# The last output pair and the first two feed-forward blocks issued in written order on ScalarE and VectorE

## The chip, the cores and the metric

One core of one Trainium2 chip runs the whole layer in one launch. The metric is the device time of an execution in microseconds; the times before are 1346.68, 1347.53 and 1349.25 us, median 1347.53.

## The reference

One encoder layer on 1024 tokens of width 1024, all in float32. After two kinds of attention and a gated sum, the part that matters here is:

```python
x = x + y @ w_out                                    # the "output" product
h = rms_norm(x, norm_ffn)
u = silu(h @ w_gate) * (h @ w_up)                    # 2816 hidden columns
x = x + u @ w_down
```

## The kernel before

**Products.** Each float32 operand is split in two: `split` lets ScalarE round the source to the fast matmul type (the high part, line 50 or, with a scale, 53) and VectorE subtract (the low part, line 51 or 54). A product is three matmuls, high x high, high x low and low x high (lines 788 to 790). Two 256-wide pieces of weights are multiplied at once by a Strassen-Winograd scheme with seven products, numbered 1 to 7 (class `Seven`). Each product is one `step`: 12 matmuls of 128x512. A step needs its weights (`prepare`: a sum of weight quarters on VectorE, line 765, then a split) and four token operands `mv[p][0..3]`. Its result goes to one of four PSUM banks X, Y, V and Z. Steps 1 and 6 end with a ScalarE copy of one bank into the next (line 792), because later steps add onto that copy: Y is copied to Z after step 6, and steps 7, 3 and 4 follow, 7 and 4 into Z and 3 into Y.

**Output pairs.** `out_pair(i)`, i = 0 to 3, computes 256 rows of x @ w_out in order 1, 5, 6, 2, 7, 3, 4 (pair 0 in another order). It adds the banks to two residual rows `r[i,0]` and `r[i,1]` (lines 1074 and 1096), stores them to x1_dram and adds up squares for the norm. It also makes the token sums that the feed-forward products take (`TokenSums`: t1, t2, t3 early, t4 in `rest`). Their two buffers hold one pair at a time, so the sums of pairs 0 to 2 go to f_dram, six rows of 256 KB each. Four buffers of tag e4 hold the residual rows of two pairs less one, and the running squares. The rows of pair i+1 are loaded in step 4 of pair i, one before and one after the six stores.

**Feed-forward blocks.** `hidden(i)`, 22 of them, each takes one 128-column piece of w_gate and w_up through the same seven steps. Blocks 0 and 1 run interleaved in order 1, 5, 6, 7, 3, 2, 4. After step 6 of both, `ffn_norm` sums the squares on TensorE, VectorE and GpSimd make 1/rms, and after step 7 `spread_norm` spreads it over the partitions. Their token operands for products 5, 6, 7, 3, 2 and 4 (that is `BACK`, index n) are made by `feed(n, j)`, j being the pair: j < 3 is fetched from f_dram into the low half of the operand's slot and split there, j = 3 is split from the sums on chip. `first_feeds` issues the twelve fetches of n = 0 to 3 in step 2 of pair 3; n = 4 and 5 follow after the pair. Slots have tags: products 5 and 6 take U slots (used before by the output operands 1 and 5), 7 and 3 take V slots (before: 6 and 2), 2 and 4 take H slots (before: 7, 3, 4).

**Order of issue.** TensorE follows the written order throughout. `dma` keeps all loads and stores of these stages in written order on the SyncE queue, which waits in turn for each slot or value. ScalarE and VectorE follow a planner that reorders by estimated times; in step 2 of pair 3 the weights of products 1 and 5 of blocks 0 and 1 get a higher priority.

Of the kernel before, what the change touches and what calls it, by code (L numbers as in the profile page):

```python
# [25 lines left out]
def block_kernel(ctx, tc, x, xt, small, w_in, rpb, t5, w_ba, w_bb, w_out, w_gate, w_up, w_down,  # L26
                 onehot, swmask, namask, out):
    nc = tc.nc
    P = 128
# [15 lines left out]
    def f(ap):  # L45
        return ap.bitcast(F32)

    def split(hi, lo, src, eng=None, scale=None):
        if scale is None:
            a = nc.scalar.copy(hi, src)  # L50
            b = (eng or nc.vector).tensor_tensor(lo, src, f(hi), ALU.subtract)  # L51
        else:
            a = nc.scalar.activation(hi, src, AF.Copy, scale=scale)
            b = nc.vector.scalar_tensor_tensor(lo, src, scale, f(hi), op0=ALU.mult, op1=ALU.subtract)
        return a.ins, b.ins
# [18 lines left out]
    def operand(tag, nm):  # L74

        z = big.tile([P, 2, 512], F32R, tag=tag, name=nm, bufs=16 if tag == "H" else 8)
        return z[:, 0, :], z[:, 1, :]
# [9 lines left out]
    def dma(dst, src):  # L87

        tc.keep_in_program_order(nc.sync.dma_start(dst, src))
# [4 lines left out]
    def half_cols(h):  # L94
        return slice(h * 512, h * 512 + 512)

    def tok(t):
        return slice(t * P, (t + 1) * P)
# [74 lines left out]
    f_dram = drp.tile([18 * P, 512], F32, name="f_dram")  # L173
# [303 lines left out]
    with tc.tile_pool(name="at", bufs=1) as ap:  # L477
# [144 lines left out]
        n = len(steps)  # L622
# [40 lines left out]
        for gi, (kind, _) in enumerate(order):  # L663
            m = 8 * group_columns(*order[gi])[1]
            lo, hi = due[gi], due[gi + 1]
# [35 lines left out]
    ORDER = (1, 5, 6, 2, 7, 3, 4)  # L701
# [6 lines left out]
    def scratch(nm):  # L708
        return hp.tile([P, 512], F32, tag="S", name=nm, bufs=2)
# [4 lines left out]
    def scratch2(nm):  # L714
        return hp.tile([P, 1024], F32, tag="e4", name=nm, bufs=4)
# [12 lines left out]
    def in_turn(*gens):  # L728
        gens = list(gens)
        while gens:  # L730
            gens = [g for g in gens if next(g, gens) is not gens]

    def bank_sets():

        return [{b: bank(RING[4 * i + n], f"bank{b}{i}") for n, b in enumerate("XYVZ")} for i in range(2)]
# [133 lines left out]
    sets = bank_sets()  # L869
# [77 lines left out]
    sets = bank_sets()  # L947
# [12 lines left out]
    for n, (d, half) in enumerate(turns):  # L960
        j, c = d // 2, half_cols(half)
# [15 lines left out]
        if half == 0:  # L977
            p = 2 if d % 2 else 1
# [4 lines left out]
            elif d == 7:  # L983
                my[7], my[3] = ([operand("H", f"y{p}_{i}") for i in range(4)] for p in (7, 3))
                for m, q in enumerate((7, 3)):
                    for i in range(3):
                        hi, lo = my[q][i]
                        row = (3 * m + i) * P
                        dma(f(lo), y_dram[row:row + P, :])
                        split(hi, lo, f(lo))  # L990
        elif d % 2:
            (b11, b12), (b21, b22) = halves(y[d - 1]), halves(y[d])
            t = TokenSums(f"y{j}", b11, b12, b22).rest(b21)
# [3 lines left out]
            for m, p in enumerate((7, 3, 4)):  # L997
                row = (3 * m + j) * P
# [7 lines left out]
    for q in (7, 3, 4):  # L1006
        for i in range(4) if q == 4 else (3,):
            hi, lo = my[q][i]
            if i < 3:
                row = (6 + i) * P  # L1010
# [3 lines left out]
    hid = {}  # L1014

    def prefetch_ffn(i):

        if i >= NF:
            return prefetch_down(i - NF)
        st = [w_stage(f"wg{i}_"), w_stage2(f"wu{i}_")]  # L1020
        for t, w in zip(st, (w_gate, w_up)):
            dma(t.rearrange("p (k c) -> p k c", c=P), w[0, :, tok(i)].rearrange("(k p) c -> p k c", p=P))
        hid[i] = Seven(f"f{i}", [two(z) for z in st], 4, mx, sets)
# [18 lines left out]
    mx = {1: [operand("H", f"f1_{j}") for j in range(4)]}  # L1042
    r = {}

    def out_row(i, a):
        r[i, a] = scratch2(f"r{i}_{a}")
        dma(r[i, a], xt[tok(2 * i + a), :])
# [4 lines left out]
    raw_t = {}  # L1052
    pairs = {0: loads}
    BACK = (5, 6, 7, 3, 2, 4)

    def feed(n, j):

        hi, lo = mx[BACK[n]][j]
        src, scale = raw_t[j][BACK[n]]
        if j < 3:  # L1060
            row = (3 * n + j) * P
            dma(f(lo), f_dram[row:row + P, :])
            src = f(lo)
        split(hi, lo, src, scale=scale)

    def out_pair(i, order, then={}):
        s = pairs[i]
        ra = r[i, 0], r[i, 1]
        x, y, v, z = (s.banks[b] for b in "XYVZ")
        ga, gb = (gffn[:, 2 * i + a:2 * i + a + 1] for a in range(2))  # L1070

        def done(a, half, bank_):
            c = half_cols(half)
            nc.vector.tensor_add(ra[a][:, c], bank_, ra[a][:, c])
            dma(x1_dram[tok(2 * i + a), c], ra[a][:, c])

        def squares(a, half):
            c = half_cols(half)
            if i or (a, half) not in ((0, 0), (1, 1)):
                sq = scratch(f"sq{i}_{a}_{half}")  # L1080
                nc.scalar.activation(sq, ra[a][:, c], AF.Square)
                nc.vector.tensor_add(both_sums[:, c], both_sums[:, c], sq)
            else:
                nc.scalar.activation(both_sums[:, c], ra[a][:, c], AF.Square)

        for p in order:
            s.prepare(p)
        for p in order:
            s.step(p)
            if p == 2:  # L1090
                done(0, 0, x)
                split(*mx[1][i], ra[0][:, LO], scale=ga)
                squares(0, 0)
            elif p == 5:
                for a in range(2):
                    nc.vector.tensor_add(ra[a][:, HI], v, ra[a][:, HI])
            elif p == 7:
                done(1, 1, z)
                squares(1, 1)
            elif p == 3:  # L1100
                done(0, 1, y)
                t = raw_t[i] = TokenSums(f"x{i}", ra[0][:, LO], ra[0][:, HI], ra[1][:, HI], ga, gb)
                if i == 3:
                    for n in range(4):
                        feed(n, 3)
                squares(0, 1)
            elif p == 4:
                done(1, 0, z)
                t.rest(ra[1][:, LO])
                if i < 3:  # L1110
                    out_row(i + 1, 0)
                    for n, q in enumerate(BACK):
                        row = (3 * n + i) * P
                        dma(f_dram[row:row + P, :], t[q][0])
                    out_row(i + 1, 1)
                squares(1, 0)
            then.get(p, lambda: None)()

    def prefetch_out(i):
        pairs[i] = out_loads(i)  # L1120

    def first_feeds():
        for n in range(4):
            mx[BACK[n]] = [operand("UUVV"[n], f"f{BACK[n]}_{j}") for j in range(4)]
            for j in range(3):
                feed(n, j)

    prefetch_out(1)
    for i in range(3):
        order = ORDER if i else FIRST  # L1130
        out_pair(i, order, {order[3]: lambda: prefetch_out(i + 2) if i < 2 else prefetch_ffn(0)})
    def lead_in():
        prefetch_ffn(1)
        with tc.high_priority(offset=400):
            for p in (1, 5):
                for i in range(2):
                    hid[i].prepare(p)
        first_feeds()

    out_pair(3, ORDER, {2: lead_in})  # L1140


    mv = mx
    for n in (4, 5):
        mx[BACK[n]] = [operand("H", f"f{BACK[n]}_{j}") for j in range(4)]
        for j in range(4):
            feed(n, j)

    rsb = wide_rs

    def ffn_norm(half, ss):

        for j in range(4):
            nc.tensor.matmul(ss[:, j:j + 1], both_sums[:, tok(4 * half + j)], ones[:, 0:1], start=True, stop=True)
        rs = hp.tile([P, 4], F32, tag="rs", name=f"rs{half}", bufs=2)
        nc.vector.tensor_scalar(rs, ss[:, 0:4], 1.0 / D, EPS, op0=ALU.mult, op1=ALU.add)  # L1156
        nc.gpsimd.tensor_tensor(rs, rs, mhalf[:, 0:4], ALU.pow)  # L1157
        dg = scratch(f"dg{half}")
        for j in range(4):
            nc.vector.tensor_scalar_mul(dg[:, tok(j)], ident, rs[:, j:j + 1])  # L1160
        return dg

    def spread_norm(half, dg, rb):
        for j in range(4):
            nc.tensor.matmul(rb[:, tok(j)], ones, dg[:, tok(j)], start=True, stop=True)
        nc.scalar.copy(rsb[half], rb)
# [42 lines left out]
            nc.sync.dma_start(u_dram[row:row + P, :], t[p][0])  # L1209

    ga, gb = (hidden(i, LAST2) for i in range(2))
    for g in (ga, gb, ga, gb, ga, gb):
        next(g)
    dg = [ffn_norm(half, sets[half]["V"]) for half in range(2)]
    next(ga)
    next(gb)
    for half in range(2):
        spread_norm(half, dg[half], sets[half]["V"])
    in_turn(ga, gb)
    for i in range(2, NF - 2):  # L1220
        run(hidden(i))
# [6 lines left out]
    for ch, (k0, n) in enumerate(CHUNKS):  # L1228
        for q, p in enumerate(ORDER):
            for j in range(n):  # L1230
                hi, lo = mv[p][j]
                row = (7 * (k0 + j) + q) * P
# [92 lines left out]
```

## Time and profile before

| | us |
|---|---|
| median of three runs | 1347.53 |
| profiled execution | 1350.09 |
| its span, first to last instruction | 1348.30 |
| TensorE busy in the span | 1316.1 |
| VectorE, ScalarE busy | 1005.4, 673.4 |

The span is what the rows below are measured in; 1.79 us of the profiled execution lie outside it. The profiled execution is 2.56 us above the median of the three runs. Times of a row are counted from the span's start. TensorE has work for 98% of the span, so a time saved is an idle stretch of TensorE filled, or a stretch at its lower clock brought to the higher.

### The profile page before, as it was taken

How to read it: one execution, taken by the hardware profiler on the slowest of the kernel's cores; microseconds unless marked ns; L12 is line 12 of the kernel's file. 1: busy time of each engine (PE TensorE's matmuls, PEld its weight loads, DVE VectorE, ACT ScalarE, POOL GpSimd, SP SyncE). 2: the span in 40 equal slices, each digit the busy share in tenths (PEclk: the TensorE clock that was granted, in tenths of full speed). 3: DMA queues.
4: the chain of work that ended last, by engine and by line, in shares of the span. 5: the costliest groups of instructions: out<-in, count | busy, mean ns of one | idle time of the engine just before them, and what ended most of it. 6: DMA issues, size and time to landing. Idle time of an engine off the chain costs nothing.

```text
span 1348.3 us, 19145 instructions
## 1 busy us (share of the span) xinstructions
PE 1316.1 (98%) x6464; PEld 1132.6 (84%) x6464; DVE 1005.4 (75%) x1989; ACT 673.4 (50%) x1381; POOL 170.6 (13%) x308
## 2 busy tenths in 40 slices
PE   9999999999999999999997999999999999999998
PEld 8999999999887887887885888888888888888887
DVE  5678878887769736768978867766667679797775
ACT  7567857776645224535555433333333347263432
POOL 1354645563210000000000000000000000000000
PEclk9999999999999999999998999999999999999999
DMA  9431312142514436657783433223333346682542
GB/s 327 120 86 41 95 54 82 44 116 55 170 66 152 141 94 202 202 176 226 241 288 105 132 101 102 86 88 109 117 118 111 96 139 225 243 262 65 165 133 86
DMA packets 177571, 184.03 MB, mean 136 GB/s; under 512 B 20496, under 2 KB 125968, under 8 KB 177472
## 3 DMA queue, kind: packets, MB, share of 16 engines
q1 hardware_dynamic: 177216, 182.70, 42.9%
q8 instruction: 51, 0.84, 0.3%
q14 instruction: 48, 0.39, 0.1%
q10 hardware_dynamic: 256, 0.10, 0.0%
HBM read 128.74 MB, written 48.97 MB: 132 GB/s over the span
## 4 chain that ended last, share of the span: by engine, by line
PE 84%; DVE 7%; DMA 4%; ACT 3%; issue 2%; SPq 1%; POOL 0%; ACTq 0%; DVEq 0%; POOLq 0%
PE bankZ L788 6%; PE bankZ L790 6%; PE bankZ L789 6%; PE bankY L790 5%; PE bankY L788 5%; PE bankY L789 5%; PE bankX L789 5%; PE bankX L790 5%; PE bankX L788 5%; PE pj L317 4%; PE pj L316 4%; PE pj L315 4%; PE bankV L789 3%; PE o L602 3%; PE bankV L790 3%; PE bankV L788 3%
## 5 line engine op out<-in xcount | busy, mean ns | idle before, releaser
L552 ACT ACTIVATE E<-E,nm 128x384 f32<-128x384 f32 (+3 forms) x128 | 75.7, 591 | 51.6 <-DVE nm L546 46.0
L554 POOL TENSOR_SCALAR E<-E,nm 128x384 f32<-128x384 f32 (+1 forms) x128 | 78.1, 611 | 101.3 <-DVE nm L553 72.0
L51 DVE TENSOR_TENSOR pl<-tp,ph 128x384 fp32r<-128x384 f32 (+1 forms) x128 | 66.3, 518 | 13.4 <-ACT ph L50 12.2
L50 ACT CAST ph<-tp 128x384 fp32r<-128x384 f32 (+1 forms) x128 | 57.4, 449 | 21.6 <-PE tp L564 20.6
L51 DVE TENSOR_TENSOR f<-f 128x512 fp32r<-128x512 f32 x89 | 58.3, 684 | 10.4 <-ACT f L50 10.3
L50 ACT CAST f<-f 128x512 fp32r<-128x512 f32 x89 | 52.6, 617 | 25.6 <-DMA f<-u_dram 21.6
L564 PE MATMUL tp<-ident,E 128*128 128x128 f32 x352 | 59.6, 272 | 0.1
L602 PE MATMUL o<-pl,v 128*128 128x256 f32 (+2 forms) x160 | 49.1, 307 | 3.0 <-DVE pl L51 2.9
L335 POOL TENSOR_TENSOR ss<-ss,mhalf 128x4 f32<-128x4 f32 (+2 forms) x42 | 49.4, 1176 | 3.1
L564 PEld LDWEIGHTS tp<-ident,E 128*128 128x128 f32 x352 | 45.3, 140 | 5.2 <-POOL E L554 0.3
L602 PE MATMUL o<-ph,v 128*128 128x256 f32 (+2 forms) x160 | 46.2, 303 | 2.2 <-DVE of L585 2.1
L540 PE MATMUL s<-k,q 128*128 128x384 f32 (+1 forms) x128 | 46.5, 363 | 1.3 <-DVE nm L546 1.3
L1171 ACT ACTIVATE sg<-sg 128x512 f32<-128x512 f32 x44 | 27.8, 632 | 35.3 <-DVE sg L1170 35.3
L1157 POOL TENSOR_TENSOR rs<-rs,mhalf 128x4 f32<-128x4 f32 x2 | 2.0, 1014 | 341.9 <-DVE rs L1156 341.9
L541 PE MATMUL s<-k,q 128*128 128x384 f32 (+1 forms) x128 | 41.3, 323 | 0.0
L790 PE MATMUL bankV<-f,f_5l 128*128 128x512 f32 x88 | 35.1, 399 | 4.0 <-DVE f_5l L51 4.0
L546 DVE CUSTOM_DVE_ANT_0 E<-s,bsw,cols 128x384 f32<-128x384 f32 (+1 forms) x64 | 36.8, 576 | 2.8 <-PE s L541 2.2
L546 DVE CUSTOM_DVE_ANT_0 E<-s,bna 128x384 f32<-128x384 f32 (+1 forms) x64 | 33.0, 517 | 6.0 <-PE s L541 5.5
L790 PE MATMUL bankY<-f,f_6l 128*128 128x512 f32 x88 | 35.1, 399 | 2.2 <-DVE f_6l L51 2.2
L788 PE MATMUL bankV<-f,f_5h 128*128 128x512 f32 x88 | 34.9, 397 | 2.4 <-ACT f_5h L50 2.4
L553 DVE RECIPROCAL nm<-nm 128x1 f32<-128x1 f32 x128 | 20.2, 159 | 22.5 <-ACT E L552 21.2
L51 DVE TENSOR_TENSOR f_2l<-wg_s,f_2h 128x512 fp32r<-128x512 f32 x22 | 15.1, 690 | 28.6 <-ACT f_2h L50 28.6
(800 smaller groups left out, 4538.9 us busy)
## 6 DMA issues: line engine op xcount, KB each, us to landing
f<-u_dram SPq DMA_DIRECT2D x77, 256.0 KB
wg_s<-in_w_gate_dram SPq DMA_DIRECT2D x22, 512.0 KB
u_dram<-uT SPq DMA_DIRECT2D x33, 256.0 KB
sg<-g_dram SPq DMA_DIRECT2D x32, 256.0 KB
g_dram<-go SPq DMA_DIRECT2D x24, 256.0 KB
u_dram<-tau SPq DMA_DIRECT2D x22, 256.0 KB
u_dram<-tbu SPq DMA_DIRECT2D x22, 256.0 KB
f<-f_dram SPq DMA_DIRECT2D x18, 256.0 KB
```

Of the source, the lines that this page charges most:

```text
L50: a = nc.scalar.copy(hi, src)
L51: b = (eng or nc.vector).tensor_tensor(lo, src, f(hi), ALU.subtract)
L315: nc.tensor.matmul(ps[:, :384], lh, his[k][:, :384], start=(k == 0), stop=False)
L316: nc.tensor.matmul(ps[:, :384], lh, los[k][:, :384], start=False, stop=False)
L546: nc.vector.tensor_tensor_reduce(E[:, :n], s[:, :n], hd["bias"](qb), -1.0, sk if sw else 1e30, ALU.add, ALU.min, nm[:, 0:1])
L552: nc.scalar.activation(E[:, :m], E[:, :m], AF.Exp, bias=nm[:, 0:1], scale=-1.0, accum_out=nm[:, 1:2])
L554: nc.gpsimd.tensor_scalar(E[:, :n], E[:, :n], nm[:, 1:2], 1.0, op0=ALU.mult, op1=ALU.mult)
L564: nc.tensor.transpose(tp[:, tok(j)], hd["E"][qq][:, ko:ko + P], ident)
L602: nc.tensor.matmul(hd["O"][half][:, (a - half * 4) * P:(z + 1 - half * 4) * P], v[:, kb].rearrange("p a e -> p (a e)"), pp[:, (a - q0) * P ...
L788: nc.tensor.matmul(ps, hi[:, tok(j)], bh, start=first, stop=False, skip_group_check=True)
L789: nc.tensor.matmul(ps, hi[:, tok(j)], bl, start=False, stop=False, skip_group_check=True)
L790: nc.tensor.matmul(ps, lo[:, tok(j)], bh, start=False, stop=end, skip_group_check=True)
```

## The change

Four edits. The residual rows of the next pair are loaded earlier (steps 2 and 3 in place of step 4). The row j = 2 of products 5, 6 and 7 is split from the sums still on chip (`kept`), which drops three stores and three fetches. Fetches and splits are separate functions: fetches of n = 0, 1, 2, 3 are issued in steps 1, 5, 6 and 2 of pair 3, those of n = 4 and 5 in step 4, and block 1's weights are loaded ahead of all these. And from there until `change.close()`, ScalarE and VectorE issue in written order, with each split and weight sum given a place.

```diff
+    def kept(n, j):
+        return j == 3 or j == 2 and n < 3
+    def fetch(*what):
+        for n, j in what:
+            mx.setdefault(BACK[n], {})[j] = operand("UUVVHH"[n], f"f{BACK[n]}_{j}")
+            if not kept(n, j):
+                row = (3 * n + j) * P
+                dma(f(mx[BACK[n]][j][1]), f_dram[row:row + P, :])
+    def feed(*what):
+        for n, j in what:
+            hi, lo = mx[BACK[n]][j]
+            src, scale = raw_t[j][BACK[n]]
+            split(hi, lo, src if kept(n, j) else f(lo), scale=scale)
...
         for p in order:
             s.prepare(p)
+        then.get(0, lambda: None)()
...
             if p == 2:
...
+                if i < 3:
+                    out_row(i + 1, 0)
...
                 if i == 3:
-                    for n in range(4):
-                        feed(n, 3)
+                    add_up_ffn(2)
+                    feed((0, 3), (1, 3))
+                    prepare_ffn((0, 6), (1, 6))
                 squares(0, 1)
+                if i < 3:
+                    out_row(i + 1, 1)
             elif p == 4:
...
                 if i < 3:
-                    out_row(i + 1, 0)
                     for n, q in enumerate(BACK):
                         row = (3 * n + i) * P
-                        dma(f_dram[row:row + P, :], t[q][0])
-                    out_row(i + 1, 1)
+                        if not kept(n, i):
+                            dma(f_dram[row:row + P, :], t[q][0])
...
-    def lead_in():
-        prefetch_ffn(1)
-        with tc.high_priority(offset=400):
-            for p in (1, 5):
-                for i in range(2):
-                    hid[i].prepare(p)
-        first_feeds()
-    out_pair(3, ORDER, {2: lead_in})
+    def begin():
+        prepare_ffn((0, 1))
+        prefetch_ffn(1)
+        change.enter_context(tc.manual_schedule(engines={mybir.EngineType.Activation, mybir.EngineType.DVE}))
+    out_pair(3, ORDER, {
+        0: begin,
+        1: lambda: fetch((0, 0), (0, 1), (0, 2), (0, 3)),
+        5: lambda: (fetch((1, 0), (1, 1), (1, 2), (1, 3)), feed((0, 2), (0, 0), (0, 1))),
+        6: lambda: (hid[0].add_up(1), fetch((2, 0), (2, 1), (2, 2), (2, 3)), feed((1, 2), (1, 0)), prepare_ffn((0, 5))),
+        2: lambda: (fetch((3, 0), (3, 1), (3, 2), (3, 3)), prepare_ffn((1, 1)), hid[1].add_up(1)),
+        7: lambda: (feed((1, 1), (2, 2), (2, 0)), prepare_ffn((1, 5))),
+        4: lambda: (add_up_ffn(3), feed((2, 3), (2, 1)), fetch(*((n, j) for n in (4, 5) for j in range(4)))),
+    })
...
-    for g in (ga, gb, ga, gb, ga, gb):
-        next(g)
-    dg = [ffn_norm(half, sets[half]["V"]) for half in range(2)]
-    next(ga)
-    next(gb)
+    both_blocks()
+    for i, g in enumerate((ga, gb)):
+        prepare_ffn((i, 7))
+        next(g)
+    add_up_ffn(4)
+    feed(*((3, j) for j in range(4)))
+    for i, g in enumerate((ga, gb)):
+        prepare_ffn((i, 3))
+        next(g)
+    rs = [ffn_norm(half, sets[half]["V"]) for half in range(2)]
+    feed(*((4, j) for j in range(4)))
+    dg = [diagonal(half, rs[half]) for half in range(2)]
+    both_blocks()
+    prepare_ffn((0, 2), (1, 2))
     for half in range(2):
         spread_norm(half, dg[half], sets[half]["V"])
+    feed(*((5, j) for j in range(4)))
+    change.close()
     in_turn(ga, gb)
```

## Rows read from the trace of the kernel before

**Rows 1.** Stretches: us, busy of PE, PEld, DVE, ACT, POOL, clock, DMA, GB/s.

```profile
700.00:800.00 100.00, 91.39 (x403) 75.03 (x402) 81.23 (x138) 49.78 (x86) 2.03 (x2) 0.95 0.39 127
680.92:699.96 19.04, 19.04 (x86) 15.77 (x84) 10.96 (x19) 5.92 (x10) 0.00 (x0) 1.00 0.75 251
705.40:728.89 23.49, 14.88 (x50) 11.11 (x49) 21.22 (x35) 14.60 (x27) 0.00 (x0) 0.78 0.34 122
```

**Rows 2.** Waits of TensorE, 700 to 800 us: total, times, longest.

```profile
PE bankV L790 <- DVE f_5l L51: 4.0, 1, 4.0
PE bankV L788 <- ACT f_5h L50: 2.4, 1, 2.4
PE bankY L790 <- DVE f_6l L51: 2.2, 1, 2.2
```

**Rows 3.** Instructions of TensorE in order of time: start us, us, idle before.

```profile
691.80 0.39 PE L788 MATMUL bankZ<-y,o_7h 128*128 128x512 f32 x1
697.24 0.39 PE L788 MATMUL bankZ<-y,o_4h 128*128 128x512 f32 x1
705.40 0.39 PE L788 MATMUL bankV<-f,f_5h 128*128 128x512 f32 x1
715.38 0.79 PE L790 MATMUL bankV<-f,f_5l 128*128 128x512 f32 x1 [4.00 <-DVE f_5l L51]
718.53 0.50 PE L788 MATMUL bankV<-f,f_5h 128*128 128x512 f32 x1
728.89 1.84 PE L1154 MATMUL bankV<-ones,sums 128*128 128x1 f32 x16
```

**Rows 4.** Instructions of ScalarE in order of time.

```profile
689.28 0.57 ACT L792 COPY bankZ<-bankY 128x512 f32<-128x512 f32 x1 [4.64 <-PE bankY L790]
700.09 1.41 ACT L53 ACTIVATE f<-f,cols 128x512 fp32r<-128x512 f32 x2 [0.76 <-DMA f<-f_dram]
738.16 0.62 ACT L50 CAST f_1h<-wg_s 128x512 fp32r<-128x512 f32 x1 [0.30 <-DMA wg_s<-in_w_gate_dram]
```

**Rows 5.** Instructions of VectorE in order of time.

```profile
694.05 0.69 DVE L1096 TENSOR_TENSOR r<-bankV,r 128x512 f32<-128x512 f32 x1 [1.36 <-DMA r<-in_xt_dram]
703.51 0.74 DVE L54 SCALAR_TENSOR_TENSOR f<-f,cols 128x512 fp32r<-128x512 f32 x1
704.17 0.68 DVE L51 TENSOR_TENSOR f_5l<-s1f,f_5h 128x512 fp32r<-128x512 f32 x1
704.77 0.68 DVE L765 TENSOR_TENSOR s1f<-wu__7949 128x512 f32<-128x512 f32 x1
723.42 0.69 DVE L51 TENSOR_TENSOR f_6l<-s2f,f_6h 128x512 fp32r<-128x512 f32 x1 [0.69 <-ACT f_6h L50]
725.40 0.69 DVE L51 TENSOR_TENSOR f_7l<-s3f,f_7h 128x512 fp32r<-128x512 f32 x1 [0.68 <-ACT f_7h L50]
```

**Rows 6.** DMA issues of SyncE in order of time: start us, us of issue.

```profile
677.59 6.18 SPq L89 DMA_DIRECT2D x_dram<-r  x3
683.86 0.38 SPq L89 DMA_DIRECT2D r<-in_xt_dram  x1
688.50 0.57 SPq L89 DMA_DIRECT2D r<-in_xt_dram  x1
692.72 0.32 SPq L89 DMA_DIRECT2D x_dram<-r  x1
694.65 7.83 SPq L89 DMA_DIRECT2D f<-f_dram  x12
734.38 0.38 SPq L89 DMA_DIRECT2D wg_s<-in_w_gate_dram  x1
```

**Rows 7.** Stretches for the DMA traffic, columns as in Rows 1.

```profile
684.00:687.00 3.00, 3.00 (x15) 2.49 (x14) 1.29 (x3) 0.64 (x2) 0.00 (x0) 1.00 0.76 213
687.00:692.00 5.00, 5.00 (x23) 4.13 (x23) 0.69 (x1) 0.57 (x1) 0.00 (x0) 1.00 1.05 404
695.00:699.00 4.00, 4.00 (x19) 3.34 (x18) 3.30 (x6) 2.07 (x4) 0.00 (x0) 1.00 1.09 304
```

More of the change, by code (lines that the diff above doesn't have):

```diff
@@ L1054, in block_kernel, with prepare_ffn, add_up_ffn @@
     BACK = (5, 6, 7, 3, 2, 4)
[L1056 to L1064, printed above, removed]
+    def kept(n, j):
[11 more added lines that the diff above has]
+            split(hi, lo, src if kept(n, j) else f(lo), scale=scale)
+    def prepare_ffn(*what):
+        for i, p in what:
+            hid[i].prepare(p)
+    def add_up_ffn(*which):
+        for i in range(2):
+            hid[i].add_up(*which)
     def out_pair(i, order, then={}):
@@ L1120, in prefetch_out @@
         pairs[i] = out_loads(i)
[L1122 to L1126, printed above, removed]
     prefetch_out(1)
@@ L1131, in block_kernel @@
         out_pair(i, order, {order[3]: lambda: prefetch_out(i + 2) if i < 2 else prefetch_ffn(0)})
-    def lead_in():
+    change = ExitStack()
+    def begin():
+        prepare_ffn((0, 1))
         prefetch_ffn(1)
-        with tc.high_priority(offset=400):
-            for p in (1, 5):
-                for i in range(2):
-                    hid[i].prepare(p)
-        first_feeds()
-    out_pair(3, ORDER, {2: lead_in})
+        change.enter_context(tc.manual_schedule(engines={mybir.EngineType.Activation, mybir.EngineType.DVE}))
[8 more added lines that the diff above has]
+    })
     mv = mx
[L1144 to L1147, printed above, removed]
     rsb = wide_rs
@@ L1157, in ffn_norm, with diagonal @@
         nc.gpsimd.tensor_tensor(rs, rs, mhalf[:, 0:4], ALU.pow)
+        return rs
+    def diagonal(half, rs):
         dg = scratch(f"dg{half}")
@@ L1211, in block_kernel, with both_blocks @@
     ga, gb = (hidden(i, LAST2) for i in range(2))
-    for g in (ga, gb, ga, gb, ga, gb):
-        next(g)
-    dg = [ffn_norm(half, sets[half]["V"]) for half in range(2)]
-    next(ga)
-    next(gb)
+    def both_blocks():
+        next(ga)
+        next(gb)
+    both_blocks()
+    for i, g in enumerate((ga, gb)):
+        prepare_ffn((i, 7))
+        next(g)
+    add_up_ffn(4)
[8 more added lines that the diff above has]
+    prepare_ffn((0, 2), (1, 2))
     for half in range(2):
         spread_norm(half, dg[half], sets[half]["V"])
+    feed(*((5, j) for j in range(4)))
+    change.close()
     in_turn(ga, gb)
```

## The prediction

> **What bounds the kernel now.** I read the stretches first. TensorE is busy for all 19.04 us of pair 3 at full clock, but for 91.39 of the 100 us from 700 to 800, at a mean clock of 0.95 [rows 1]. The waits of TensorE in that stretch are three: 4.0, 2.4 and 2.2 us, for operands of products 5 and 6 that VectorE and ScalarE make [rows 2]. So the whole room lies between the first matmul of product 5 of block 0 (705.40) and the norm's first matmul (728.89): 23.49 us [rows 3]. In it stand 4 steps of 12 matmuls. A step's pace is read from steps 7 and 3 of pair 3: 24 matmuls from 691.80 to 697.24, 0.2267 us each, 2.72 us a step [rows 3]. Four steps are 10.88 us, so 12.6 us are lost: 8.6 idle and about 4 at the lower clock (0.78 granted in this stretch; after the wait of 4.00, the matmuls from 715.38 to 718.53 run at the 1.2 GHz level) [rows 1 to 3]. The cause is visible in VectorE: 21.22 of 23.49 us busy there, against 10.96 of 19.04 in pair 3 just before [rows 1]. Its work comes in a heap because the fetched rows are issued at 694.65 and land from 700.09 on [rows 4, 6].
>
> **The change, part by part.** *What goes.* If every operand is ready, all 12.6 us go; that is the upper bound.
>
> *Loads of residual rows moved up.* Two 512 KB loads per pair move ahead of other DMAs on SyncE. VectorE waited up to 1.36 us for one [rows 5] with TensorE busy, so the gain is nothing. The cost is on the queue. The second load now waits in step 3 until row r[i,0] is stored (three stores stand in the 6.18 us from 677.59 [rows 6]), and everything behind it waits too. In pair 2 this decides the rest, see below.
>
> *Three stores and three fetches dropped.* 6 x 262 KB less traffic; at 404 GB/s [rows 7] 0.65 us of queue each. The three stores stand ahead of the first fetch, so 2 us earlier; counted in the sum below.
>
> *Where the first fetch now stands on SyncE.* In order: second load r[3,1]; store (1,0) of pair 2; three f_dram stores; two weight loads of block 1; then rows (0,0) and (0,1). The first of these waits for the store (0,1) of pair 2. VectorE makes that value near 679, inside those 6.18 us; its data now moves behind the other 512 KB load, 1.3 us at 404 GB/s, so I put its completion, and SyncE free, at 683.9 (681 to 684.7 possible). That is where the burst of before starts too (the third store ends the 6.18 us and so is issued near 683.5, then r at 683.86) [rows 6]. How long a burst takes is read from two places. From the store at 683.5 to the landing of r[3,1] at 694.05: 10.5 us for a store, two residual rows and six f_dram stores, 2.88 MB. From the store at 692.72 to the landing of the first row at 700.09: 7.4 us for a store, two weight loads and a row, 1.57 MB [rows 4 to 6]. The line through both is 3.6 us + 2.4 us per MB. In the changed kernel the DMAs up to row (0,0) are 0.52 + 0.26 + 0.79 + 1.05 + 0.26 = 2.88 MB, so 10.5 us, and weights move at about 304 instead of 404 GB/s [rows 7], 0.85 us more for 1.05 MB: between 694.4 and 695.3. I take 695.0. Early bound: SyncE free at 681, so that r[3,1] goes alone before the store at 683.5, and the other 2.36 MB by the line from there: 692.8. Late bound: the first 1.57 MB at 213 GB/s (7.4 us), weights at 304 (3.5 us), the row (0.65), 1.5 us to land, from 684.7: 697.7.
>
> A rule of the Trainium skill speaks to this place. DMA: Bandwidth & Descriptors, section Queues, rings and completion order, says that each DMA engine consumes descriptors in ring order; the first row's 5.4 us from issue to landing behind 1 MB of weights, against 3.8 us for a 512 KB load alone (734.38 to 738.16), agrees [rows 4, 6]. By the same page's section Anatomy of one DMA, whose fit of about 2.0 us plus bytes at 436 GB/s is for GpSimd's path and a DMA by itself, the row would land 2.6 us after an issue near 687.4, at 690.0, and the sum would be a gain of 10.5 us. No run here shows a row landing that soon.
>
> *Written order on ScalarE: a new wait.* In written order the splits (0,2), (0,0), (0,1) come in step 5, ahead of the copy Y to Z that ends step 6. Before, that copy ran at 689.28, and step 7 started at 691.80 [rows 3, 4]. Now it stands behind two casts of rows that land at 695.0 and 0.65 us later: the copy starts near 696.2 and ends at 696.8. Step 7, which adds onto Z, starts 5.0 us late. Behind the cast on ScalarE wait this copy and all later splits; behind the subtraction on VectorE wait the residual additions.
>
> *VectorE after that.* From the subtraction of (0,0) (start 695.7, one cast later) to that of (0,3), the last operand of product 5, the written order has 24 VectorE instructions: 8 row splits, 3 weight splits, the split of product 1, 3 residual additions, 3 token sums, 2 sums of squares and 4 of weights. At 0.60 us (704.17 to 704.77) for 18 plain ones and 0.66 (703.51 to 704.17) for 6 scaled ones [rows 5] that is 14.8 us; for waits on ScalarE inside it (split of product 1, two squares) I add 2.0, an estimate from three casts of 0.6 to 0.7 us. So it ends at 712.5. TensorE, 5.0 us late, wants product 5 at 705.4 + 5.0 = 710.4, or 712.0 if it pays 1.6 us at the lower clock as 715.38 to 718.53 does (8 matmuls at about 0.43) [rows 3]. VectorE ends last in either case, so the clock costs nothing more. Product 5 starts at 712.5; four steps bring the norm to 723.4 instead of 728.89: a gain of 5.5 us.
>
> *Norm and later.* Between norm and spread VectorE must place 4 splits and the diagonals, about 4.4 us, beside two steps of 5.4 us: hidden, bounds 0 to +2 us. Fetches of n = 3, 4, 5 are issued before 716 and used after 718: hidden. The weights of block 2 move by the same few us and were cast at 738.16 [rows 4], many steps before use: hidden. The dropped high priority only concerns weights that now have a place.
>
> *Sum.* 12.6 - 7.1 (the late start of product 5, 712.5 against 705.4) = 5.5 us. From the profiled execution's 1350.09: 1344.6. That execution is 2.56 us above the median of the runs; against 1347.53 it is 1342.0. With the landing bounds 692.8 and 697.7 the gain is 7.7 to 2.8: 1339.8 to 1344.8.
>
> **The rivals.** *Rows in time (0.20).* The row lands as a load alone does, at most 3.8 us after an issue at 687.4 [rows 4, 6], or the copy is not held behind the casts. A landing at 691.2 gives a gain of 9.3 us, one before 688 all 12.6: 1335 to 1339, 1337 in the middle. For it: fewer bytes, and the DMA was nearly idle until 684. Against it: the two loads of before that queued took 5.4 and 5.5 us. The fit on the skill's page belongs to this case.
>
> *The gain given back (0.17).* Each us of later landing costs one us, because both chains start there. At 700.5 nothing is left; a landing from 697.8 to 703.2 leaves the time within 2.7 us of before: 1347.5 in the middle. For it: traffic after a pause moved at only 213 GB/s [rows 7]. Against it: it needs more than the late bound.
>
> *Cast and subtraction in step with each other (0.13), slower.* Where the two engines alternate, a split costs 2.0 us of VectorE's time (723.42 to 725.40, idle 0.69 in each) in place of about 1.2 for sum and subtraction [rows 5]; the written order gives no other work to fill in. The price is 0.75 us a split. From 8 of the 15 such splits up to product 6's the gain is gone, and with 12 to 15 it is slower by 3.5 to 5.8 us: 1351 to 1353. For it: each wait in a written order holds everything behind it, on two engines that wait for each other and for TensorE. Against it: the weight sums stand several instructions ahead of their casts.
>
> **How the numbers follow.** The forecast has 0.50 (1339.8 to 1344.8, its own range). Each rival as given. The predicted time is 1342.0. The range from 1335.0 to 1350.0 leaves out the slower case and the last bit of the full gain. About 0.2% (2.7 us) is what a measurement of this kernel can tell from no change: faster is the forecast and the first rival, 0.70; within 0.2%, 0.17; slower, 0.13.
>
> **What would show it.** Right: in pair 3, TensorE waits before its first matmul of step 7 (bank Z, line 788) for the ScalarE copy of line 792, some 5 us; ScalarE waits for f<-f_dram just before that copy, until about 695; product 5 of block 0 starts near 712 with its last wait on VectorE; no wait of 4 us stands in products 5 and 6; the norm's first matmul is near 723. The rows (0,0) landing before 690 and no wait at step 7 would mean the first rival. VectorE idle 0.7 us before most of its subtractions would mean the last. The forecast is wrong if a wait longer than 1 us stands after the norm, or the queue is not what releases the copy.

## The result and the profile after

The changed kernel takes 1336.7 us (median of 6 runs, 1335.58 to 1338.31) against 1347.65 us of the kernel before beside it (6 runs, 1346.68 to 1350.01). The ratio is 0.9917, with a 95% interval from 0.9904 to 0.9929. The forecast was 1342.0: the change gains 10.95 us, twice the 5.5 of the forecast's sum, and lands in the case of the first rival, "Rows in time" (1335 to 1339). The profiled execution took 1337.31 us, its span 1335.5.

The first view is again the waits of TensorE, here from 660 to 760 us, total, times and longest. The three waits of [rows 2] are gone and a short one stands ahead of step 4 of pair 3.

```profile
PE bankZ L788 <- DVE r L1090: 1.1, 1, 1.1
```

TensorE in order of time in the changed kernel (start, us, idle before in brackets), as in [rows 3]: the first matmuls of steps 1, 7 and 4 of pair 3, of product 5 of block 0, and of the norm.

```profile
678.97 0.39 PE L788 MATMUL bankX<-y,o_1h 128*128 128x512 f32 x1
...
689.85 0.39 PE L788 MATMUL bankZ<-y,o_7h 128*128 128x512 f32 x1
...
696.60 0.50 PE L788 MATMUL bankZ<-y,o_4h 128*128 128x512 f32 x1 [1.15 <-DVE r L1090]
...
704.93 0.39 PE L788 MATMUL bankV<-f,f_5h 128*128 128x512 f32 x1
...
715.92 1.84 PE L1171 MATMUL bankV<-ones,sums 128*128 128x1 f32 x16
```

From step 1 of pair 3 to the norm TensorE has 13 steps, 35.36 us at 2.72. Before they took 728.89 - 680.92 = 47.97 us, so 12.61 were lost; now they take 36.95, so 1.59 are lost. 11.02 us come from this one place. From the norm to the end of the span it is 619.41 us before and 619.58 after: nothing was given back behind it. The 1.95 us by which step 1 itself is early are not counted. 1.6 of them stand at the start of pair 0 already, ahead of the first edit: the first matmul of line 782 is at 618.5 us before and at 616.9 after (the other one of each line is that of pair 1), and in another execution of the changed kernel (e10 below) it is at 618.8.

```profile
L782 PE MATMUL bankY<-y x2: 389/389/389, 618.5 to 642.2; 128*128 128x512 f32 x2
L782 PE MATMUL bankY<-y x2: 389/389/389, 616.9 to 640.4; 128*128 128x512 f32 x2
```

The stretches, with the columns of [rows 1], show the same: TensorE is busy for all of 700 to 800 at a granted clock of 1.00 (before: 91.39 us and 0.95), and VectorE is even fuller from product 5 to the norm than it was (10.95 of 10.99 us, before 21.22 of 23.49 [rows 1]), but TensorE has no wait for it there.

```profile
700.00:800.00 100.00, 100.00 (x458) 83.19 (x457) 83.69 (x143) 49.11 (x85) 2.87 (x2) 1.00 0.39 120
704.93:715.92 10.99, 10.99 (x49) 8.93 (x48) 10.95 (x19) 8.47 (x18) 0.00 (x0) 1.00 0.49 167
```

Where the forecast went astray is seen on SyncE. Its DMA issues in order of time (start, us of issue; xN is N DMAs), to be set beside [rows 6]:

```profile
674.80 2.74 SPq L89 DMA_DIRECT2D x_dram<-r  x2
679.84 1.00 SPq L89 DMA_DIRECT2D f<-f_dram  x2
681.57 0.33 SPq L89 DMA_DIRECT2D r<-in_xt_dram  x1
681.99 0.38 SPq L89 DMA_DIRECT2D f<-f_dram  x1
682.47 0.38 SPq L89 DMA_DIRECT2D x_dram<-r  x1
682.90 0.42 SPq L89 DMA_DIRECT2D f_dram<-g22x  x1
683.38 0.47 SPq L89 DMA_DIRECT2D f_dram<-r  x1
683.89 0.90 SPq L89 DMA_DIRECT2D f<-f_dram  x1
684.89 0.98 SPq L89 DMA_DIRECT2D f_dram<-tbx  x1
685.91 0.78 SPq L89 DMA_DIRECT2D wg_s<-in_w_gate_dram  x1
686.89 0.95 SPq L89 DMA_DIRECT2D wu__7891<-in_w_up_dram  x1
687.95 3.32 SPq L89 DMA_DIRECT2D f<-f_dram  x2
```

In written order the load of r, the store of x, three f_dram stores and both weights come first and the rows f<-f_dram after them. The queue of the changed kernel is another: rows (0,0) and (0,1) go out at 679.84, (1,0) at 681.99 and (1,1) at 683.89, and the weights follow at 685.91. So on ScalarE (next fence, in order of time) the splits of the rows start at 683.20 without a wait, and the copy Y to Z at 687.33 waits for TensorE alone, as in [rows 4].

```profile
683.20 1.33 ACT L53 ACTIVATE f<-f,cols 128x512 fp32r<-128x512 f32 x2
687.33 0.57 ACT L792 COPY bankZ<-bankY 128x512 f32<-128x512 f32 x1 [2.80 <-PE bankY L790]
```

VectorE in order of time: the second residual addition waits 1.60 us for r[3,1], which now stands behind the rows on SyncE, and with it everything up to the addition at 695.85 that step 4 needs. That is the 1.15 us wait that is left.

```profile
686.90 0.69 DVE L1115 TENSOR_TENSOR r<-bankV,r 128x512 f32<-128x512 f32 x1 [1.60 <-DMA r<-in_xt_dram]
...
688.17 1.41 DVE L54 SCALAR_TENSOR_TENSOR f<-f,cols 128x512 fp32r<-128x512 f32 x2
...
695.85 0.69 DVE L1090 TENSOR_TENSOR r<-bankZ,r 128x512 f32<-128x512 f32 x1
...
704.31 0.74 DVE L54 SCALAR_TENSOR_TENSOR f<-tax,cols,f 128x512 fp32r<-128x512 f32 x1
```

### The profile page after: what moved, and what is told of

Same layout as the page of the kernel before. It is cut to its first block, busy times and chain, and to the rows that moved or that the text cites. A ratio compares the mean times of both kernels' runs of the same rounds, so it can differ in the third digit from the quotient of the medians.

```text
span 1335.5 us, 19127 instructions
## 1 busy us (share of the span) xinstructions
PE 1311.2 (98%) x6464; PEld 1130.1 (85%) x6464; DVE 1005.3 (75%) x1989; ACT 673.9 (50%) x1381; POOL 170.5 (13%) x308
## 4 chain that ended last, share of the span: by engine, by line
PE 83%; DVE 6%; DMA 6%; ACT 2%; issue 2%; SPq 1%; POOL 0%; ACTq 0%; DVEq 0%
PE bankZ L788 6%; PE bankZ L789 6%; PE bankZ L790 6%; PE bankY L788 5%; PE bankY L790 5%; PE bankY L789 5%; PE bankX L789 5%; PE bankX L788 5%; PE bankX L790 5%; PE pj L316 3%; PE pj L315 3%; PE pj L317 3%; PE o L602 3%; PE bankV L789 3%; PE bankV L790 3%; PE bankV L788 3%
## 5 line engine op out<-in xcount | busy, mean ns | idle before, releaser
L602 PEld LDWEIGHTS o<-pl,v 128*128 128x128 f32 x160 | 30.1, 188 | 5.6 <-DVE pl L51 4.9
L50 ACT CAST f_5h<-s1f 128x512 fp32r<-128x512 f32 x22 | 13.7, 621 | 41.4 <-DVE s1f L765 38.2
L1211 DVE TENSOR_TENSOR sg<-bankY,p 128x512 f32<-128x512 f32 x22 | 15.2, 691 | 25.7 <-PE bankY L790 25.7
```

The lines of the kernel that those rows point to most:

```text
L602: nc.tensor.matmul(hd["O"][half][:, (a - half * 4) * P:(z + 1 - half * 4) * P], v[:, kb].rearrange("p a e -> p (a e)"), pp[:, (a - q0) * P ...
```

## Experiments

All ratios are to the kernel before, run on the same chip beside each kernel. "Stretch" is the time from the matmul of line 782 into bank Y in pair 1 to the norm's first matmul, in the one profiled execution of each: 86.7 us before, 75.5 in the changed kernel. It leaves out what differs between executions elsewhere.

| kernel | written order, ScalarE and VectorE | rows (0,0), (0,1) ahead of the weights | row (1,0) too | j = 2 on chip | us | ratio, 95% | stretch |
|---|---|---|---|---|---|---|---|
| e2 | no | no | no | yes | 1349.89 | 1.0015 [1.0006, 1.0024] | 87.8 |
| e3 | yes, copy first | no | no | yes | 1348.66 | 1.0005 [0.9997, 1.0014] | 87.1 |
| e1 | yes | no | no | yes | 1345.78 | 0.9981 [0.9972, 0.9991] | 81.8 |
| e6 | no | yes | no | yes | 1346.55 | 0.9985 [0.9976, 0.9994] | 84.4 |
| e5 | yes | yes | no | yes | 1345.81 | 0.9974 [0.9964, 0.9983] | 82.9 |
| e8 | yes | yes | no | no | 1346.63 | 0.9985 [0.9976, 0.9994] | 84.3 |
| e9 | yes | yes | yes | yes | 1340.05 | 0.9942 [0.9927, 0.9956] | 76.2 |
| changed, again (e10) | yes | yes | yes | yes | 1338.22 | 0.9928 [0.9915, 0.9942] | 76.1 |
| e7, and again (e11) | yes, splits first | yes | yes | yes | 1338.62, 1337.83 | 0.9926 [0.9913, 0.9938], 0.9921 [0.9908, 0.9934] | 74.5, 74.8 |
| e4 | yes, sum later | yes | yes | yes | 1336.43 | 0.9914 [0.9900, 0.9927] | 75.2 |
| e12 | yes, both | yes | yes | yes | 1337.25 | 0.9917 [0.9903, 0.9931] | 74.5 |

**e1: the changed kernel with SyncE in written order.**

```diff
+    queue = ExitStack()
+    queue.enter_context(tc.manual_schedule(engines={mybir.EngineType.SP}))
     prefetch_out(1)
...
     change.close()
+    queue.close()
```

> The changed kernel, but SyncE's DMAs from the output pairs to the spread norm are also held in written order, so that the first two fetched rows stand behind the last residual row, four stores and the two weight loads of block 1, as the prediction had assumed. Theory Q (the gain hangs on the two rows being issued ahead of these, as the trace after shows): they land near 695 on the old time scale, step 7 of pair 3 waits 4 to 5 us for ScalarE's copy, product 5 starts about 5 to 7 us late, and the time is 1342, 5.5 us above the changed kernel. Rival W (the written order of ScalarE and VectorE brings it all, where the rows stand in the queue is indifferent): 1336.7, no new wait at step 7.

Measured: 1345.78 us (1343.83 to 1348.88, 11 runs). This is the kernel that the prediction had in mind, and its mechanism is there up to the stop at step 7. SyncE issues the rows at 687.76, behind the weights:

```profile
685.79 0.91 SPq L89 DMA_DIRECT2D wg_s<-in_w_gate_dram  x1
686.74 0.98 SPq L89 DMA_DIRECT2D wu__7893<-in_w_up_dram  x1
687.76 5.09 SPq L89 DMA_DIRECT2D f<-f_dram  x6
```

ScalarE waits 10.39 us for them, and the copy stands behind:

```profile
694.95 1.40 ACT L53 ACTIVATE f<-f,cols 128x512 fp32r<-128x512 f32 x2 [10.39 <-DMA f<-f_dram]
696.26 0.58 ACT L792 COPY bankZ<-bankY 128x512 f32<-128x512 f32 x1
```

TensorE waits for that copy at step 7, starts product 5 at 712.44 and the norm at 723.49:

```profile
696.89 0.80 PE L788 MATMUL bankZ<-y,o_7h 128*128 128x512 f32 x1 [5.61 <-ACT bankZ L792]
...
712.44 0.39 PE L788 MATMUL bankV<-f,f_5h 128*128 128x512 f32 x1
...
723.49 1.84 PE L1173 MATMUL bankV<-ones,sums 128*128 128x1 f32 x16
```

From 640 to 770 us that is TensorE's only wait; none stands at product 5. Behind the stop it runs at a lower granted clock for a while (stretches, columns as in [rows 1], clock third from the end):

```profile
PE bankZ L788 <- ACT bankZ L792: 5.6, 1, 5.6
697.00:705.00 8.00, 8.00 (x28) 6.25 (x29) 6.51 (x12) 4.04 (x8) 0.00 (x0) 0.79 0.43 140
705.00:712.00 7.00, 7.00 (x33) 5.78 (x32) 6.86 (x12) 4.38 (x8) 0.00 (x0) 1.00 0.19 73
```

The profiled execution (1344.87) is 5.2 us under the profiled one of before, near the 5.5 of the sum. The median is only 2.2 us under that of the kernel before beside it (1347.97), so the 1342 of the expectation was missed by 3.8 us; the rival's 1336.7 is ruled out. The runs of e1 lie 5 us apart, and by the prediction's chain each us of later landing costs one; that the landing is what differs between them is argued, not shown, since one run has a trace. What follows: the place of the rows in SyncE's queue decides most of the gain.

**e2: the changed kernel with the planner on ScalarE and VectorE.**

```diff
-        change.enter_context(tc.manual_schedule(engines={mybir.EngineType.Activation, mybir.EngineType.DVE}))
```

> The changed kernel with ScalarE and VectorE left to the planner (everything else of the change stays; SyncE then stands in written order too). Theory W: without the written order the heap comes back, TensorE loses about 12 us again in products 5 and 6: 1347. Theory Q: rows late as in the run with the queue in written order, but the planner lets other work pass, so 3 to 6 us are lost in place of 12.6: 1339.5 to 1342.5.

Measured: 1349.89 us, 1.0015 of before: all that was gained is gone, and a little more. SyncE stands in written order again here (rows at 686.59, behind the weights at 685.34 and 685.84), so this run undoes two things at once. With the planner the copy is not held (687.56), but the work of products 1 and 5 comes in a heap as before: TensorE in order of time, its two waits in product 5, at the place of those of [rows 2].

```profile
713.28 0.79 PE L788 MATMUL bankV<-f,f_5h 128*128 128x512 f32 x1 [6.46 <-ACT f L53]
...
717.92 0.79 PE L789 MATMUL bankV<-f,f_5h 128*128 128x512 f32 x1 [3.85 <-DVE f L54]
```

Removed stores, earlier loads and weights, left to the planner, are worth nothing together. The figure of 1339.5 to 1342.5 (theory Q) missed, and the 1347 of theory W is 2.9 us short.

**e3: e1, with the splits of the fetched rows behind the copy.**

```diff
-        5: lambda: (fetch((1, 0), ...), feed((0, 2), (0, 0), (0, 1))),
-        6: lambda: (hid[0].add_up(1), ...
+        5: lambda: fetch((1, 0), ...),
+        6: lambda: (feed((0, 2), (0, 0), (0, 1)), hid[0].add_up(1), ...
```

> The queue in written order as in the first run, and the splits of rows (0,2), (0,0), (0,1) placed behind the copy of step 6 in place of ahead of it. The prediction's account (two chains start at the landing, ScalarE's copy and 24 VectorE instructions, and VectorE's ends last): the wait at step 7 goes, a wait on VectorE stands before step 4 or product 5 in its place, the time stays at that of the first run within 1 us (1342). Rival (only the held copy costs): the time comes down to 1337 to 1338.

Measured: 1348.66 us. The wait moved as expected, from step 7 to step 4, where TensorE waits for the residual addition behind those splits on VectorE. The time missed the expectation by more than 5 us, and it is 2.9 us above that of e1. TensorE, order of time:

```profile
706.49 0.80 PE L788 MATMUL bankZ<-y,o_4h 128*128 128x512 f32 x1 [10.22 <-DVE r L1090]
...
717.48 0.39 PE L788 MATMUL bankV<-f,f_5h 128*128 128x512 f32 x1
```

The norm is 4.9 us later than in e1. The rows landed 2.4 us later (697.31 against 694.95); and the three steps from 706.49 took 10.99 us where 36 matmuls at 0.2267 take 8.16, so 2.83 went to the lower clock, which the stretches show (columns as in [rows 1]):

```profile
700.00:708.00 8.00, 1.51 (x4) 1.22 (x5) 6.51 (x12) 3.90 (x7) 0.00 (x0) 0.50 0.46 164
708.00:716.00 8.00, 8.00 (x28) 6.39 (x27) 7.86 (x13) 4.89 (x9) 0.00 (x0) 0.73 0.09 33
```

So moving the wait past the copy is no cure; only earlier rows are.

**e4: the changed kernel, with block 1's split for product 1 and its first weight sum moved from step 2 to step 7.**

```diff
-        2: lambda: (fetch((3, 0), ...), prepare_ffn((1, 1)), hid[1].add_up(1)),
-        7: lambda: (feed((1, 1), ...
+        2: lambda: fetch((3, 0), ...),
+        7: lambda: (prepare_ffn((1, 1)), hid[1].add_up(1), feed((1, 1), ...
```

> The changed kernel with the weight split of product 1 of block 1 and a weight sum moved behind VectorE's residual addition of step 7. Theory: the last wait of TensorE in this stage (1.15 us before step 4, for that addition) goes, 1335.6. Rival: the wait only moves on to product 5 or 6: 1336.7, with a wait of about 1 us there.

Measured: 1336.43 us, ratio 0.9914 [0.9900, 0.9927], the same as the changed kernel. The wait of 1.15 us is gone and another of 1.0 us stands in its place, ahead of product 6, for a ScalarE copy, as the rival had it. The times of theory and rival (1335.6, 1336.7) lie too close for the medians to tell apart. What is left of the loss doesn't hang on this piece of work alone. The waits of TensorE:

```profile
PE bankY L788 <- ACT bankY L792: 1.0, 1, 1.0
```

**e5: all three engines written (e1's lines are in too), with the rows (0,0), (0,1) put ahead.** Behind them in step 1 come r[3,1], the last stores of pair 2 (one x store and three f_dram stores, collected in `later`) and block 1's weights.

```diff
+    def behind_rows():
+        out_row(3, 1)
+        for dst, src in later:
+            dma(dst, src)
+        prefetch_ffn(1)
...
-        1: lambda: fetch((0, 0), (0, 1), (0, 2), (0, 3)),
+        1: lambda: (fetch((0, 0), (0, 1), (0, 2), (0, 3)), behind_rows()),
```

> Written order on all three, SyncE too, but the two rows (0,0) and (0,1) are written ahead of the last residual row, of pair 2's last four stores and of block 1's weights, which all move behind them. Theory Q (only the rows' place in the queue separated the first run of the queue in written order from the changed kernel): rows land near 683 to 685, no stop at step 7, 1336.5 to 1338. Rival (the written queue costs in another place, later loads for instance): 1342 to 1346.

Measured: 1345.81 us, where theory Q had 1336.5 to 1338 and the rival 1342 to 1346. The stop at step 7 is gone (copy at 687.97), but the next row, (1,0), is now the one behind the weights, and ScalarE waits 6.80 us for it (order of time):

```profile
684.29 1.37 ACT L53 ACTIVATE f<-f,cols 128x512 fp32r<-128x512 f32 x2 [0.35 <-DMA f<-f_dram]
687.97 0.57 ACT L792 COPY bankZ<-bankY 128x512 f32<-128x512 f32 x1 [2.31 <-PE bankY L790]
688.45 0.63 ACT L50 CAST f<-tax 128x512 fp32r<-128x512 f32 x1
695.88 0.62 ACT L50 CAST f<-f 128x512 fp32r<-128x512 f32 x1 [6.80 <-DMA f<-f_dram]
```

Behind it on VectorE waits the addition that step 4 needs. The waits of TensorE:

```profile
PE bankZ L788 <- DVE r L1091: 6.3, 1, 6.3
```

**e6: e5's queue with the planner on ScalarE and VectorE** (e5's edit and e2's, without e1's lines; SyncE still issues the rows at 682.24, r[3,1] at 684.08 and the weights at 688.18).

> The same place of the rows in the queue, with ScalarE and VectorE left to the planner. Theory: the gain needs both parts, early rows and the order of the splits; the planner still puts these splits behind other work, the heap returns, 1346 to 1350. Rival: early rows alone bring most of it, 1337 to 1340.

Measured: 1346.55 us, norm at 727.20, waits of 3.7 us at step 4 and 2.5 in product 5, as its theory had it (1346 to 1350). Early rows without the written order don't do it either.

**e7: the changed kernel, with the splits (0,2), (0,0), (0,1) moved up from step 5 to step 1.**

```diff
-        1: lambda: fetch((0, 0), ...),
-        5: lambda: (fetch((1, 0), ...), feed((0, 2), (0, 0), (0, 1))),
+        1: lambda: (fetch((0, 0), ...), feed((0, 2), (0, 0), (0, 1))),
+        5: lambda: fetch((1, 0), ...),
```

> The changed kernel with the three splits (0,2), (0,0), (0,1) written in step 1, ahead of the two residual additions of step 5, of which the second waits on VectorE 1.60 us for its row. Theory: VectorE's sequence starts about 1.9 us earlier, the wait of 1.15 us before step 4 and the one that took its place when that was removed both go, 1335.1 (at most 1.6 us can still be won in this stage). Rival: the wait comes back elsewhere, 1336.7.

Measured: 1338.62 us, ratio 0.9926. No wait of TensorE stands from 640 to 770 us, and the stretch is 1.0 us shorter than in the changed kernel. The time is above both the theory's 1335.1 and the rival's 1336.7, and the ratio doesn't show the 1.0 us: the changed kernel had 0.9917, on another chip.

**e8: the changed kernel with row j = 2 stored and fetched again.**

```diff
-        return j == 3 or j == 2 and n < 3
+        return j == 3
```

> The changed kernel with the three rows j = 2 of products 5, 6 and 7 stored and fetched again instead of split from the sums on chip. Theory Q: row (0,2), first in the written order, now stands in the queue behind stores and the weight loads, lands near 695, and holds the copy as in the first run: 1345 to 1348, with a stop of 5 us or more at step 7. Rival (three transfers of 0.65 us, hidden): 1336.7 to 1338.

Measured: 1346.63 us, within the 1345 to 1348 of the theory that it bears out; TensorE stops for 7.9 us at step 7. Rows (0,0) and (0,1) go out at 679.75, but the first split of the written order is now a fetched row behind the weights. ScalarE:

```profile
695.38 1.95 ACT L53 ACTIVATE f<-f,cols 128x512 fp32r<-128x512 f32 x3 [13.02 <-DMA f<-f_dram]
697.24 0.58 ACT L792 COPY bankZ<-bankY 128x512 f32<-128x512 f32 x1
```

TensorE's only wait from 640 to 770 us:

```profile
PE bankZ L788 <- ACT bankZ L792: 7.9, 1, 7.9
```

The rows (1,0) and (1,1) went out behind the weights here as well (688.59), so this run prices both together; but the first wait, 13.02 us long, is for the row that the changed kernel keeps. So the three fetches dropped count less as traffic than because the split that stands first in written order needs no DMA.

**e9: e5, with the rows (1,0), (1,1) ahead of the stores and weights as well.** The lines are set against e5; `behind_rows` has no `out_row` here.

```diff
-        1: lambda: (fetch((0, 0), ...), behind_rows()),
-        5: lambda: (fetch((1, 0), ...), feed((0, 2), (0, 0), (0, 1))),
+        1: lambda: (fetch((0, 0), ...), out_row(3, 1)),
+        5: lambda: (fetch((1, 0), ...), behind_rows(), feed((0, 2), (0, 0), (0, 1))),
```

> The kernel with all three engines in written order and the rows of product 5 ahead of the big transfers, but with the rows of product 6 put there too: rows (0,0), (0,1) and the load of r[3,1] in step 1 of pair 3, rows (1,0), (1,1) in step 5, and behind these the last stores of pair 2 and the weights of block 1. Theory (the gain hangs on the place of both pairs of rows in SyncE's queue, and on nothing else that the planner did there): no wait for an operand of products 5 and 6 over 1.5 us, first matmul of product 5 to the norm and the stretch before it as in the changed kernel, 75 to 76 us from block 1's side to the norm; ratio to the kernel before 0.990 to 0.993 (1336 to 1339). Rival (putting the rows early only moves the wait on to the next row or to the weights, as it did with product 5's rows alone): one wait of 3 to 6 us in products 6 or 7, norm near 720 or later, ratio 0.996 to 0.998 (1343 to 1346).

Measured: 1340.05 us (1338.82 to 1342.13), ratio 0.9942 [0.9927, 0.9956]; norm at 717.45. All three engines are in written order here, and the rows alone have been moved in the queue: the stretch is 76.2 us against 76.1 of the changed kernel on that chip. The time is nearer to the theory (0.990 to 0.993) than to the rival (0.996 to 0.998), though just outside it; the changed kernel's interval there overlaps. SyncE, order of time:

```profile
680.62 1.00 SPq L89 DMA_DIRECT2D f<-f_dram  x2
683.87 0.33 SPq L89 DMA_DIRECT2D r<-in_xt_dram  x1
684.29 0.86 SPq L89 DMA_DIRECT2D f<-f_dram  x2
```

The wait that is left is that of the changed kernel, for the addition behind r[3,1]; the operands of products 5 and 6 make no wait:

```profile
PE bankZ L788 <- DVE r L1091: 1.8, 1, 1.8
```

**e10, e11, e12: the changed kernel and e7 again, and e7 with e4's edit, on one chip.**

> The changed kernel itself once more, beside the next one on the same chip. Both theories: ratio to the kernel before 0.990 to 0.993, norm near 716, one wait of about 1 us for the residual addition before step 4 of pair 3.

> The changed kernel with the splits (0,2), (0,0), (0,1) in step 1 of pair 3, ahead of the residual additions, timed beside the changed kernel itself. Theory (the stretch up to the norm is 1.0 us shorter in the profile, and nothing behind it gives that back): ratio 0.0005 to 0.0012 below that of the changed kernel (0.6 to 1.6 us). Rival (given back elsewhere, or too small to see): the two ratios differ by less than 0.0005.

> The kernel of the run before with the weight sum of block 1's product 1 moved from step 2 to step 7 as well, ahead of the splits there. Theory (both moves only take VectorE work away from the residual additions, and TensorE has no wait left in this stretch): same as the run before within 0.5 us. Rival (the later sum delays the splits of step 7): a wait of about 1 us before product 6 or 7, 0.5 to 1.5 us slower than the run before.

Measured: 1338.22, 1337.83 and 1337.25 us. The wait at step 4 of the changed kernel was 1.7 us this time. e11 is 0.0007 under e10 in the ratio, within what the theory gave (0.0005 to 0.0012), but the intervals overlap, and the first comparison of the two kernels pointed the other way. e11 has a wait of 0.5 us left at step 4; e12 is within 0.6 us of e11, with a wait of 0.3 us. In the profiles these moves take 1.0 to 1.6 us off the stretch (74.5 in e7 and e12, against 75.5 and 76.1 in the two executions of the changed kernel); that this makes a faster kernel than the changed one is not shown.

## Why the prediction was right and wrong

The range from 1335.0 to 1350.0 holds the measured 1336.7 because it takes in the first rival; the forecast's own range (1339.8 to 1344.8) doesn't, and its central step failed. Part by part:

*What goes (12.6 us): right.* The 13 steps lost 12.61 us before and lose 1.59 now.

*Where the first fetch now stands on SyncE: this step failed.* It put the rows behind r[3,1], four stores and both weights, as the code has them, for an issue near 687.4 and a landing at 695.0. The changed kernel issues them at 679.84. Written out so, as in e1, they are issued at 687.76 and split at 694.95. That the queue keeps written order, as is said of `dma` above, was read from the kernel before [rows 6], where it does; it also does in e2, with the planner on ScalarE and VectorE. In the changed kernel, with those two in written order, SyncE's instructions come in another order. Why the planner then puts the rows first isn't settled by these runs. In the late bound of that step, the 1.5 us to land stand in no row.

*Written order on ScalarE, a new wait: the right mechanism in a kernel that wasn't there.* e1 has the copy at 696.26 (696.2 forecast) and a wait of 5.6 us at step 7 (5.0). In the medians e1 gains 2.2 us, less than half of the forecast's 5.5.

*VectorE after that: right in length, wrong in what hangs on it.* From the subtraction of (0,0) to the end of that of (0,3) the changed kernel takes 705.05 - 688.17 = 16.9 us, and e1 takes as long; the sum was 14.8 + 2.0. But product 5 doesn't start with the end of that chain. In the changed kernel it starts at 704.93, ahead of the 705.05, and without a wait; row (0,3) is the last of the four operands of a step. In e1 too it starts (712.44) before VectorE is done with (0,3) (712.6), and no wait stands there, so the sign "its last wait on VectorE" is missing.

*The clock costs nothing more: wrong.* The reason given was that VectorE ends last. In e1 the five steps from 696.89 to 712.44 take 15.55 us for 13.60. Of these 1.95 us, 1.70 are lost by 700.63, in nine matmuls at a mean granted clock of 0.54 (1.6 was the figure set against VectorE). As TensorE waits for nothing else up to the norm, it pays stop and clock in full: 5.61 + 1.95 = 7.6 us, where the forecast had 5.0 us and then VectorE, together 7.1. That e1 has the norm at 723.49 (723.4 forecast) is luck in this part: two wrong readings nearly cancel. In e3 the 2.83 us are paid in full as well.

*Loads of residual rows moved up (no gain, a cost on the queue): a small miss.* Behind the rows r[3,1] arrives 1.60 us late for VectorE, and TensorE loses 1.15 at step 4. [rows 5] showed the same wait with slack behind it; the written order has none.

*Three stores and fetches dropped: sized wrongly.* They were counted as 2 us of queue. In e8, without them (and with the rows of product 6 behind the weights), a gain of 0.15% is left of 0.83%.

*Norm and later: right.* The stretch behind the norm is unchanged (619.41 and 619.58 us).

*The rivals.* "Rows in time" is what happened by its signs (rows before 690, no wait at step 7) and its time, but only in part for its reason. A row does land at most 3.8 us after its issue, here within 3.4; from the 687.4 that the rival kept, that would have been 691.2 and a gain of 9.3 us. What made the gain whole is the issue at 679.84, which no rival named. It was given 0.20 because both traces of a row in a queue of before spoke against it; the queue itself was not doubted. The Trainium skill (DMA: Bandwidth & Descriptors, Anatomy of one DMA) would have put the landing, by an estimate from its fit, 2.6 us after the issue. The changed kernel's at most 3.4 us leave that open; the 3.8 of e5 and e9 and the 7.2 of e1 behind 2.6 MB are longer. "The gain given back" is what e3 became, with a landing at 697.3 and not 700.5: its wait stood at step 4, and the lower clock was paid on top. "Cast and subtraction in step" didn't come: VectorE is busy for 10.95 of 10.99 us up to the norm.

## What to carry to other kernels

Where engines issue in order, read the order of the DMA queue from the instructions that are issued, and don't take it from the source: the 8 us by which the rows went out earlier (679.84 against 687.76) decided most of this gain. Small rows that an in-order engine waits for next go ahead of big loads that are needed later, and all of them, since the first row that stays behind takes the whole wait (e5, e8). And such a change is no sum of parts: kernels that lacked written order, one pair of early rows or the kept row gained 0.26% at most, and those with all of them 0.6 to 0.9%. What the earlier residual loads add by themselves is not tested.

## What the runs showed of the hardware

A 262 KB row's way from issue to the start of its split depends on what stands ahead of it in the queue: at most 3.4 us in the changed kernel, 3.8 us in e5 and e9 (680.48 to 684.29, 680.62 to 684.44, ScalarE waiting for it), but 7.2 us in e1 and e2 (687.76 to 694.95, 686.59 to 693.77), 7.2 for the second pair in e5 (688.63 to 695.88) and 8.3 in e3 (688.98 to 697.31), each behind a residual row, four stores and two weights. The Trainium skill (DMA: Bandwidth & Descriptors, Queues, rings and completion order) says that a DMA engine takes its descriptors in ring order; these rows agree.

One long stop of TensorE costs more than its length. After 5.61 us in e1 the nine matmuls from 696.89 to 700.63 take 1.70 us more than at 0.2267 us each, after 10.22 us in e3 the fifteen from 706.49 to 712.72 take 2.83 us more, both at a mean granted clock of 0.54 (a matmul at the 1.2 GHz level takes 0.43 us). After the stop of 1.15 us in the changed kernel the granted clock stays at 1.00: the step from 696.60 to 699.49 takes 2.89 us in place of 2.72, and the 0.17 us are not the clock's.
